# A hybrid transformer block on one core: a written order held longer in the first seven-product block, and x loaded ahead of the small parameters

## The chip, the cores and the metric

The kernel runs on one core of one Trainium2 chip, as one launch. The metric is the device time of that launch in microseconds (us). Five engines work side by side, each through a queue of its own: TensorE (PE, matmuls into PSUM banks), VectorE (DVE), ScalarE (ACT), GpSimd (POOL) and SyncE (SP), which here issues all DMAs. An engine takes its queue in order; an instruction that waits for a semaphore holds up all that stand behind it on that engine.

## The reference, cut to what matters

One layer of a transformer block over 512 tokens of width 1024, in float32, modulated by a condition vector `c`:

```python
mod = jax.nn.silu(c) @ w_ada[l] + b_ada[l]
sh1, sc1, g1, sh2, sc2, g2 = jnp.split(mod[:, None, :], 6, axis=-1)
hn = (_rms(x, norm1_g[l]) * (1 + sc1) + sh1).astype(x.dtype)
y = _mixer(hn, w_in[l], ...)
x = x + g1 * (y.astype(x.dtype) @ w_out[l])
hn = (_rms(x, norm2_g[l]) * (1 + sc2) + sh2).astype(x.dtype)
gate, up = jnp.split(hn @ w_gate_up[l], 2, axis=-1)
x = x + g2 * ((jax.nn.silu(gate) * up) @ w_down[l])
```

`_rms` divides each row by the root of its mean square. The mixer projects `hn` by `w_in` and runs softmax heads with a forget gate, mLSTM heads and block-sparse softmax heads. The gate and up projection has 2 x 2816 columns.

## The kernel before

Every matmul of a projection is done three times, on high and low parts of its operands: an operand is rounded by ScalarE to a high part (names that end in `h`), and VectorE subtracts that from the operand to make the low part (names in `l`).

**The start.** SP issues the loads in the order of the code: first three small ones, `c` (`cT`, 4 KB), a packed table of norm gains, biases and convolution weights (`prmT`, 44 KB) and the gate biases (`gbias`, 7 KB); then the four row tiles of x, 512 KB each (`x0` to `x3`, 128 tokens each); then the slices of `w_ada` and `w_in` for the first projection. ScalarE computes `cs`, the SiLU of `c`. The row sums of x squared are split: x0, x2 and half of x3 on ScalarE, x1 and the other half of x3 on VectorE; a chain of small VectorE instructions makes of the four sums the reciprocal roots `rs`, and both engines scale the rows by them (`xscale`). TensorE does some matmuls on `sq2`, a square of x, that are there to keep it busy, then transposes x and multiplies with `cs`.

**The gate and up projection.** It is cut into 11 blocks `q` of 256 gate columns and their 256 up columns. Block 0 is done plainly (`plain`, banks `fp`). Blocks 1 to 10 are done by a scheme that needs seven matrix products in place of eight; the seven are called phases and run in the order 1, 2, 6, 5, 7, 4, 3. A product is 24 matmuls of 256 columns. Its weights are raw tiles or sums of raw tiles: block `q` has raw tiles `r{q}00`, `r{q}01`, `r{q}11`, `r{q}10`, loaded in this order, and VectorE makes of them in place `r{q}00` (phase 5), `r{q}t` (phase 6), `r{q}01` (phase 7) and `r{q}10` (phase 4). `split` then makes `fw{q}{phase}h` on ScalarE and `fw{q}{phase}l` on VectorE. Products 6 and 7 go on accumulating in the bank `f{q}A` of phase 1, and product 3 in the bank `f{q}C` of phase 5, so each must wait until the bank has been copied or read (`u16`, `u17`, `u15`). Phases 1 and 2 of blocks 1 and 2 are done early, ahead of block 0; of these blocks five products are left. Block 0's own SiLU and product (`plain_glu`: `fps0`, `fps1` on ScalarE, `A0` on VectorE), and the last of the split operands (`os40`, `os41`), are written between the preparation of phase 7 of block 1 and what follows. `f1C` takes a bank that `fps1` reads.

**What sets the order.** A scheduler places the instructions of each engine. The class `_InOrder` (line 104) wraps each engine; while its switch `in_order[...]` is 1, each instruction gets a dependence on the one written before it, so the engine's queue keeps the written order, and while it is 0 the scheduler is free. The switches for VectorE and ScalarE are 1 through the start, then 0, and 1 again from line 1270, after block 0's matmuls. The loop over products runs the preparation two products ahead:

```python
    for i, (q, ph) in enumerate(run):
        upto = todo.index(run[min(i + AHEAD, len(run) - 1)])
        while ahead <= upto:
            prepare(*todo[ahead])
            ...
            if todo[ahead] == (1, 7):
                plain_glu(0)
                for g_ in range(2):
                    operand("s4", g_, s4[g_])
                plain_glu(1)
                in_order["V"][0] = in_order["S"][0] = 0
            ahead += 1
        product(q, ph)
        after(q, ph)
```

So before, the two switches go to 0 once phase 7 of block 1 is prepared.

Of the kernel before, what the change touches and what calls it, by code (L numbers as in the profile page):

```python
# [11 lines left out]
AF = mybir.ActivationFunctionType  # L12
ALU = mybir.AluOpType
# [3 lines left out]
P = 128  # L17
# [113 lines left out]
def hybrid_block_kernel(  # L131
# [6 lines left out]
    V, S, G, TE, SY = nc.vector, nc.scalar, nc.gpsimd, nc.tensor, nc.sync  # L138
    dbg = dbg or {}
    in_order = {k: [1] for k in "VSGTY"}  # L140
    V, S, G, TE, SY = (_InOrder(tc, e, in_order[k]) for e, k in zip((V, S, G, TE, SY), "VSGTY"))
# [33 lines left out]


    cT = cp.tile([P, 8], F32, name="cT")
    SY.dma_start(cT, c[0].rearrange("(p k) -> p k", k=8))
    prmT = cp.tile([P, NPRM], F32, name="prmT")
    SY.dma_start(prmT, prm)  # L180
    gbias = cp.tile([P, 14], F32, name="gbias")
    SY.dma_start(gbias, gate_b.partition_broadcast(P))

    cs = cp.tile([P, 8], F32, name="cs")
    S.activation(cs, cT, AF.Silu)
    b1sc = cp.tile([P, 2, 8], F32, name="b1sc")
    V.tensor_scalar(b1sc[:, 0, :], prmT[:, 8:16], 1.0, None, op0=ALU.add)
    V.tensor_scalar(b1sc[:, 1, :], prmT[:, 32:40], 1.0, None, op0=ALU.add)
    gq8 = cp.tile([P, 2], F32, name="gq8")
    V.tensor_scalar(gq8[:, 0:1], prmT[:, 84:85], -0.125, None, op0=ALU.mult)  # L190
    V.tensor_scalar(gq8[:, 1:2], prmT[:, 86:87], -0.125, None, op0=ALU.mult)

    w_ada_v = w_ada[0].rearrange("(p k) n -> p k n", k=8)

# [64 lines left out]
    with ExitStack() as s0:  # L259
# [7 lines left out]
        def load_kc(kc):  # L267

            a_ = box["ada", kc] = ap_.tile([P, 8, 2, P], F32, tag="ada", name=f"ada{kc}", bufs=ADB)
            for i in range(2):  # L270
                SY.dma_start(a_[:, :, i, :], w_ada_v[:, :, i * D + kc * P:i * D + kc * P + P])
            ws = box["ws", kc] = wp.tile([P, 512], F32, tag="ws", name=f"w0s{kc}", bufs=WS)
            SY.dma_start(ws, w_in[0, kc * P:(kc + 1) * P, MQK:MQK + 512])

        for t in range(NT):
            xx = xp.tile([P, D], F32, name=f"x{t}")
            SY.dma_start(xx, x[0, t * P:(t + 1) * P, :])
            xt.append(xx)
        for kc in range(ADB - 1):
            load_kc(kc)  # L280
        sq = [ap_.tile([P, D], F32, tag=f"sq{t % 2}", name=f"sq{t}", bufs=1) for t in range(NT)]

        def square(t, o, acc):

            if acc == "S":
                S.activation(sq[t][:, o], xt[t][:, o], AF.Square, accum_out=ss[:, t:t + 1])
            else:
                V.tensor_tensor_reduce(out=sq[t][:, o], in0=xt[t][:, o], in1=xt[t][:, o], op0=ALU.mult,
                                       op1=ALU.add, scale=1.0, scalar=0.0, accum_out=acc)

        gT = [bank("g", f"gT{m}") for m in range(4)]
        def xscale(t, c0, c1):
            if t % 2:
                S.activation(xt[t][:, c0:c1], xt[t][:, c0:c1], AF.Copy, scale=rs[:, t:t + 1])
            else:
                V.tensor_scalar(xt[t][:, c0:c1], xt[t][:, c0:c1], rs[:, t:t + 1], None, op0=ALU.mult)
# [3 lines left out]
        ssx = cp.tile([P, 1], F32, name="ssx")  # L300
        square(NT - 1, slice(0, D // 2), "S")
        square(NT - 1, slice(D // 2, D), ssx)
        V.tensor_tensor(ss[:, NT - 1:NT], ss[:, NT - 1:NT], ssx, op=ALU.add)
        V.tensor_scalar(v1, ss, 1.0 / D, EPS, op0=ALU.mult, op1=ALU.add)
        for f in rsqrt_ops(rs, v1, "n4"):
# [3 lines left out]
            TE.matmul(gT[3][:, 0:256], ident, sq[2][:, 0:256], start=True, stop=True)  # L309
        for t in range(NT):  # L310
            xscale(t, 0, XS)

        def px_(kc):
            px = box["px", kc] = bank("s", f"px{kc}")
            for t in range(NT):
                TE.transpose(px[:, t * P:(t + 1) * P], xt[t][:, kc * P:(kc + 1) * P], ident)
# [726 lines left out]
    def operand(name, g_, src):  # L1043

        mk = act_tile if name in ("22", "s1", "s3") else op_tile
        h_, l_ = (mk(f"o{name}{g_}{c}").rearrange("p (a b) -> p a b", a=2) for c in "hl")
        S.activation(h_, src, AF.Copy)
        V.tensor_tensor(l_, src, f32(h_), op=ALU.subtract)
        for i in range(2):
            so[name, 2 * g_ + i] = h_[:, i, :], l_[:, i, :]  # L1050
# [49 lines left out]
    def temp(name):  # L1100
        return act_tile(name, F32)
# [26 lines left out]
    def prepare(q, ph):  # L1128

        if ph == 1 and q + 1 < NQ:  # L1130
            load(q + 1)
        if ph in (1, 2):
            if (q, ph) not in wts:
                split(q, ph, raw[q, ph - 1, 0])
            return
        if ph == 6:
            ffn["sums"] = sums(q)
        if ph in (6, 7, 4):
            next(ffn["sums"])
        split(q, ph, {6: raw[q, "t2"], 5: raw[q, 0, 0], 7: raw[q, 0, 1], 4: raw[q, 1, 0], 3: raw[q, 1, 1]}[ph])  # L1140

    def product(q, ph):
        bk = BANK[ph]
        first = ph not in (6, 7, 3)
        if first:
            pbk[q, bk] = bank(TAG[bk], f"f{q}{bk}")
        pb = pbk[q, bk]
        for kp in range(4):
            wh, wl = wts[q, ph][kp]
            sh, sl = so[OPS[ph], kp]  # L1150
            for f in range(2):
                cs_ = slice(P * f, P * f + P)
                o = pb[:, 256 * f:256 * f + 256]
                last = kp == 3
                TE.matmul(o, wh[:, cs_], sh, start=first and kp == 0 and f == 0, stop=False, skip_group_check=True)
                TE.matmul(o, wh[:, cs_], sl, start=False, stop=False, skip_group_check=True)
                TE.matmul(o, wl[:, cs_], sh, start=False, stop=last, skip_group_check=True)
# [6 lines left out]
    def after(q, ph):  # L1164
        pb = pbk[q, BANK[ph]]
        if ph in (1, 6, 7):
            t_ = tmp[q, ph] = temp(f"u{q}{ph}")
            S.activation(t_, pb, AF.Copy)
        if ph == 2:
            V.tensor_tensor(tmp[q, 1], pb, tmp[q, 1], op=ALU.add)  # L1170
        elif ph == 7:
            pc = pbk[q, "C"]
            t_ = tmp[q, 5] = temp(f"u{q}5")
            V.tensor_tensor(t_, pc, tmp[q, 7], op=ALU.add)
        elif ph == 4:
            V.tensor_tensor(tmp[q, 7], tmp[q, 7], pb, op=ALU.subtract)
            glu(q, 1, tmp[q, 7], tmp[q, 5])
        elif ph == 3:
            V.tensor_tensor(tmp[q, 6], pb, tmp[q, 6], op=ALU.add)
            glu(q, 0, tmp[q, 1], tmp[q, 6])  # L1180
# [53 lines left out]
    def plain_glu(hb):  # L1234
        g_, u_ = pbank[hb]
        t_ = temp(f"fps{hb}")
        S.activation(t_, g_, AF.Silu)
        V.tensor_tensor(ffn["A"][0][:, :, 256 * hb:256 * hb + 256], u_.rearrange("p (a b) -> p a b", a=2),
                        t_.rearrange("p (a b) -> p a b", a=2), op=ALU.mult)
# [36 lines left out]
    def down_load(n):  # L1276
        for hf_, j in DP[len(draw):n]:
            r_ = draw[hf_, j] = fp.tile([P, 2, 512], F32, tag="raw", name=f"dr{hf_}{j}", bufs=RAW)
            SY.dma_start(r_, w_down[0, j * P:(j + 2) * P, 512 * hf_:512 * hf_ + 512].rearrange(
                "(a p) n -> p a n", p=P))  # L1280
# [15 lines left out]
    todo = [(q, ph) for q in range(1, NQ) for ph in PHASES]  # L1296
    run = [k for k in todo if k[0] > NE or k[1] > 2]
    ahead = 0
# [4 lines that stand above are left out]
            if todo[ahead] == (NQ - 1, 1):  # L1303
                down_load(4)
            if todo[ahead] == (1, 7):
                plain_glu(0)
                for g_ in range(2):
                    operand("s4", g_, s4[g_])
                plain_glu(1)
                in_order["V"][0] = in_order["S"][0] = 0  # L1310
            ahead += 1
        product(q, ph)
        after(q, ph)
# [72 lines left out]
```

## Time and profile before

| | |
|---|---|
| median of 3 runs | 685.63 us (684.65 to 687.03) |
| the profiled execution's own time | 685.51 us |
| its span in the trace | 683.8 us |
| TensorE's mean granted clock | 0.995 of full speed |
| busy: TensorE, VectorE, ScalarE, GpSimd | 650.5, 518.4, 363.9, 95.7 us |

The span is that of one execution; some 1.7 us of the time lie around it. Busy time says little about what a stage is worth: the table shows TensorE at work nearly throughout, and the places where it waits have to be looked up one by one.

### The profile page before, as it was taken

What the parts mean: (1) busy time and instruction counts of PE and PEld (TensorE: products, weight loads), DVE (VectorE), ACT (ScalarE), POOL (GpSimd) and SP (SyncE); (2) the same over time, 40 slices, a digit from 0 to 9 for tenths busy, and PEclk for the clock granted to TensorE, in tenths of its full rate; (3) what the DMA queues carried; (4) which work ended last, traced back from release to release, by engine and by line L of the source; (5) the groups of instructions that cost most, each with busy time, mean ns of one, the idle gap of its engine ahead of it and who ended that gap; (6) DMA issues with size and microseconds to landing.
All of it is one profiled execution on the core that took longest, in us unless ns stands there. A gap on an engine that the chain in (4) does not pass through costs nothing.

```text
span 683.8 us, 11780 instructions
## 1 busy us (share of the span) xinstructions
PE 650.5 (95%) x4238; PEld 587.4 (86%) x4238; DVE 518.4 (76%) x1034; ACT 363.9 (53%) x721; POOL 95.7 (14%) x130
## 2 busy tenths in 40 slices
PE   3999998999999999999996999999999999999997
PEld 2678887899999987788996999999999998788885
DVE  3539888979998899888749778887777999448313
ACT  3435487656876777637824445444544665226210
POOL 2012225245253264000000000000000000000000
PEclk9999999999999999999998999999999999999999
DMA  8986736667877776622715433223333237405101
GB/s 261 305 240 173 184 93 158 162 169 210 203 215 181 181 208 181 214 63 62 231 35 181 125 124 120 63 75 114 124 124 125 79 116 226 166 15 205 58 0 61
DMA packets 95549, 99.64 MB, mean 146 GB/s; under 512 B 8186, under 2 KB 70010, under 8 KB 95492
## 3 DMA queue, kind: packets, MB, share of 16 engines
q1 hardware_dynamic: 95492, 98.91, 49.9%
q8 instruction: 33, 0.54, 0.3%
q14 instruction: 24, 0.20, 0.1%
HBM read 84.15 MB, written 2.10 MB: 126 GB/s over the span
## 4 chain that ended last, share of the span: by engine, by line
PE 72%; DVE 15%; DMA 4%; ACT 4%; issue 4%; SPq 1%; DVEq 0%; ACTq 0%
PE d L114 14%; PE B L114 6%; PE F L114 6%; PE fp L114 3%; PE ol L114 3%; PE gT L114 3%; DVE g L114 1%; PE pc L114 1%; PE f9A L114 1%; PE f8A L114 1%; PE f7A L114 1%; PE f6A L114 1%; PE f5A L114 1%; PE f3A L114 1%; PE f4A L114 1%
## 5 line engine op out<-in xcount | busy, mean ns | idle before, releaser
L114 ACT ACTIVATE ah<-A 128x512 fp32r<-128x512 f32 x44 | 25.5, 620 | 33.4 <-PE d L114 33.1
L114 DVE TENSOR_TENSOR al<-A,ah 128x512 fp32r<-128x512 f32 x44 | 29.0, 682 | 18.1 <-ACT ah L114 18.1
L114 DVE TENSOR_TENSOR r<-r,r 128x1024 f32<-128x1024 f32 x20 | 24.3, 1219 | 9.5 <-DMA r<-in_w_gate_up_dram 9.2
L114 DVE TENSOR_TENSOR fo<-d,g1b 128x512 f32<-128x512 f32 (+1 forms) x9 | 5.6, 630 | 17.9 <-PE d L114 17.8
L114 ACT ACTIVATE Fp<-Fs,Fmn 128x128 f32<-128x128 f32 (+3 forms) x24 | 12.6, 527 | 9.6 <-DVE Fmn L114 5.6
L114 ACT ACTIVATE Bp<-Bs,Bmn 128x128 f32<-128x128 f32 (+3 forms) x24 | 12.6, 527 | 6.9 <-DVE Bmn L114 4.4
L114 DVE SCALAR_TENSOR_TENSOR m<-pc,b1sc,prmT 128x1 f32<-128x1 f32 x8 | 1.7, 218 | 19.0 <-PE pc L114 19.0
L114 POOL TENSOR_SCALAR Fp<-Fp,Fls 128x128 f32<-128x128 f32 (+2 forms) x18 | 11.9, 664 | 26.4 <-DVE Fls L114 17.2
L114 PE MATMUL gT<-sq,ident 128*128 128x256 f32 x12 | 5.1, 614 | 10.4 <-ACT sq L114 10.4
L114 ACT ACTIVATE u<-u 128x512 f32<-128x512 f32 x20 | 12.5, 626 | 2.8 <-DVE u L114 2.6
L114 DVE TENSOR_TENSOR A<-u,u 128x512 f32<-128x512 f32 x20 | 13.7, 683 | 0.0
L114 PEld LDWEIGHTS gT<-sq,ident 128*128 128x128 f32 x12 | 3.9, 331 | 11.3 <-issue 10.4
L114 POOL TENSOR_SCALAR Bp<-Bp,Bls 128x128 f32<-128x128 f32 (+2 forms) x16 | 8.7, 542 | 34.4 <-DVE Bls L114 28.1
L114 DVE TENSOR_TENSOR Bptl<-Bpt,Bpth 128x128 fp32r<-128x128 f32 (+3 forms) x24 | 11.5, 484 | 1.8 <-ACT Bpth L114 1.5
L114 DVE CUSTOM_DVE_ANT_0 Bs<-Bs,mask 128x128 f32<-128x128 f32 (+3 forms) x24 | 11.6, 491 | 1.6 <-PE Bs L114 1.5
L114 ACT ACTIVATE Fpth<-Fpt 128x128 fp32r<-128x128 f32 (+3 forms) x24 | 10.4, 435 | 4.1 <-PE Fpt L114 4.0
L114 DVE CUSTOM_DVE_ANT_0 Fs<-Fs,mask 128x128 f32<-128x128 f32 (+3 forms) x24 | 11.7, 487 | 1.0 <-PE Fs L114 1.0
L114 PE MATMUL Bpt<-ident,Bp 128*128 128x128 f32 x60 | 10.8, 277 | 1.7 <-DVE Fyp L114 0.7
L114 POOL TENSOR_TENSOR sml<-E,smh 128x512 fp32r<-128x512 f32 (+1 forms) x8 | 9.0, 1127 | 23.7 <-ACT smh L114 17.3
L114 DVE TENSOR_TENSOR Fptl<-Fpt,Fpth 128x128 fp32r<-128x128 f32 (+3 forms) x24 | 11.6, 483 | 0.6 <-ACT Fpth L114 0.4
L114 ACT ACTIVATE Bpth<-Bpt 128x128 fp32r<-128x128 f32 (+3 forms) x24 | 10.3, 434 | 3.1 <-PE Bpt L114 2.9
L114 ACT ACTIVATE row<-pc 128x256 f32<-128x256 f32 x8 | 3.1, 382 | 15.6 <-PE pc L114 15.6
(2324 smaller groups left out, 2823.9 us busy)
## 6 DMA issues: line engine op xcount, KB each, us to landing
r<-in_w_gate_up_dram SPq DMA_DIRECT2D x40, 512.0 KB, 4.6
dr<-in_w_down_dram SPq DMA_DIRECT2D x22, 512.0 KB, 5.3
ada<-in_w_ada_dram SPq DMA_DIRECT2D x16, 512.0 KB, 7.3
x<-in_x_dram SPq DMA_DIRECT2D x4, 512.0 KB, 4.6
w0s<-in_w_in_dram SPq DMA_DIRECT2D x8, 256.0 KB, 6.6
g10s<-in_w_ada_dram SPq DMA_DIRECT2D x8, 256.0 KB, 3.9
g11s<-in_w_ada_dram SPq DMA_DIRECT2D x8, 256.0 KB, 2.9
sc20s<-in_w_ada_dram SPq DMA_DIRECT2D x8, 256.0 KB, 4.1
```

What stands on the lines that cost most here:

```text
L114: r = f(*a, **k)
```

## The change

Two things. First, the switches of VectorE and ScalarE go to 0 later: not after phase 7 of block 1 but after phase 6 of block 2 is prepared, so that both engines keep the written order through the whole of block 1's five products. Second, the loads of `cT`, `prmT` and `gbias` are issued behind the four loads of x; `cs` is computed behind the squares, and the four VectorE instructions on `prmT` (`b1sc`, `gq8`) behind the first scaling.

```diff
     cT = cp.tile([P, 8], F32, name="cT")
-    SY.dma_start(cT, c[0].rearrange("(p k) -> p k", k=8))
     prmT = cp.tile([P, NPRM], F32, name="prmT")
-    SY.dma_start(prmT, prm)
     gbias = cp.tile([P, 14], F32, name="gbias")
-    SY.dma_start(gbias, gate_b.partition_broadcast(P))
...
-    S.activation(cs, cT, AF.Silu)
...
-    V.tensor_scalar(b1sc[:, 0, :], prmT[:, 8:16], 1.0, None, op0=ALU.add)
...
             SY.dma_start(xx, x[0, t * P:(t + 1) * P, :])
             xt.append(xx)
+        SY.dma_start(cT, c[0].rearrange("(p k) -> p k", k=8))
+        SY.dma_start(prmT, prm)
+        SY.dma_start(gbias, gate_b.partition_broadcast(P))
...
         square(NT - 1, slice(D // 2, D), ssx)
+        S.activation(cs, cT, AF.Silu)
...
             xscale(t, 0, XS)
+        V.tensor_scalar(b1sc[:, 0, :], prmT[:, 8:16], 1.0, None, op0=ALU.add)
...
                 plain_glu(1)
+            if todo[ahead] == (2, 6):
                 in_order["V"][0] = in_order["S"][0] = 0
```

VectorE's queue at the beginning of block 1, before (`r200` is the first sum of block 2, `r110` block 1's for phase 4):

```order
L114 TENSOR_TENSOR r1t_4877<-r111_4883,r100_4879 128x1024
L114 TENSOR_TENSOR r200_4887<-r201_4889,r200_4887 128x1024
L114 TENSOR_TENSOR r110_4885<-r1t_4877,r110_4885 128x1024
L114 TENSOR_TENSOR fw16l_4898<-r1t_4877,fw16h_4897 128x1024
L114 TENSOR_TENSOR fw15l_4902<-r100_4879,fw15h_4901 128x1024
L114 TENSOR_TENSOR r101_4881<-r111_4883,r101_4881 128x1024
L114 TENSOR_TENSOR r201_4889<-r211_4891,r201_4889 128x1024
L114 TENSOR_TENSOR fw17l_4907<-r101_4881,fw17h_4906 128x1024
```

The same place in the change, on to the first low part of block 2:

```order
L114 TENSOR_TENSOR r1t_4877<-r111_4883,r100_4879 128x1024
L114 TENSOR_TENSOR fw16l_4898<-r1t_4877,fw16h_4897 128x1024
L114 TENSOR_TENSOR fw15l_4902<-r100_4879,fw15h_4901 128x1024
L114 TENSOR_TENSOR r101_4881<-r111_4883,r101_4881 128x1024
L114 TENSOR_TENSOR fw17l_4907<-r101_4881,fw17h_4906 128x1024
...
L114 TENSOR_TENSOR fw13l_4981<-r111_4883,fw13h_4980 128x1024
L114 TENSOR_TENSOR u15_5010<-f1C_4955,u17_5008 128x512
L114 TENSOR_TENSOR r200_4887<-r201_4889,r200_4887 128x1024
L114 TENSOR_TENSOR r2t_5020<-r211_4891,r200_4887 128x1024
L114 TENSOR_TENSOR u17_5008<-u17_5008,f1D_5027 128x512
L114 TENSOR_TENSOR r201_4889<-r211_4891,r201_4889 128x1024
L114 TENSOR_TENSOR fw26l_5024<-r2t_5020,fw26h_5023 128x1024
```

`r200`, `r110` and `r201` have moved behind the low parts that stood after them; the sums of block 2 now stand behind `u15`. ScalarE's queue over the same stretch, in the change (before, `fw14h` stood between `os40h` and `os41h`, and `fw26h` and `fw25h` ahead of `u17`):

```order
L114 ACTIVATE fw17h_4906<-r101_4881 128x1024
L114 ACTIVATE fps0_4910<-fp00_4612 128x512
L114 ACTIVATE os40h_4913<-s40_4852 128x512
L114 ACTIVATE os41h_4917<-s41_4858 128x512
L114 ACTIVATE fps1_4921<-fp10_4726 128x512
L114 ACTIVATE u16_4948<-f1A_4407 128x512
L114 ACTIVATE fw14h_4951<-r110_4885 128x1024
L114 ACTIVATE fw13h_4980<-r111_4883 128x1024
L114 ACTIVATE u17_5008<-f1A_4407 128x512
L114 ACTIVATE fw26h_5023<-r2t_5020 128x1024
L114 ACTIVATE u17_5008<-u17_5008 128x512
L114 ACTIVATE fw25h_5055<-r200_4887 128x1024
```

`fw14h` comes later, `fps1` no longer has it ahead. And ScalarE's queue at the very start of the program, in the change; before, there was one table load, and `cs` stood right behind it:

```order
L114 ACT_TABLE_LOAD
L114 ACTIVATE sq_164,ss<-x_133 128x1024
L114 ACTIVATE sq_166,ss<-x_137 128x1024
L114 ACTIVATE sq_167,ss<-x_139 128x512
L114 ACT_TABLE_LOAD
L114 ACTIVATE cs<-cT 128x8
L114 ACTIVATE x_135<-x_135,rs 128x384
```

`cs` now stands between the squares and the scaling, and a second load of ScalarE's function tables has come in ahead of it. TensorE's queue changes only in which few matmuls of neighbouring products stand first; from block 4 on, no engine's order differs.

## Rows read from the trace of the kernel before

**Rows 1.** The page, busy time by engine: busy us, share of the span, instructions.

```profile
PE 650.5 (95%) x4238; PEld 587.4 (86%) x4238; DVE 518.4 (76%) x1034; ACT 363.9 (53%) x721; POOL 95.7 (14%) x130
```

**Rows 2.** Waits of TensorE, whole span: total us, times, longest us.

```profile
PE gT L114 <- ACT sq L114: 10.4, 1, 10.4
PE f1A L114 <- DVE fw16l L114: 5.5, 1, 5.5
PE ms L114 <- DMA K<-mkh: 1.4, 1, 1.4
```

**Rows 3.** Windows: length, busy us by engine, granted clock, DMA share, GB/s.

```profile
382.00:548.00 166.00, 166.00 (x1386) 166.00 (x1385) 137.91 (x145) 84.46 (x103) 0.00 (x0) 1.00 0.33 105
548.00:586.00 38.00, 37.25 (x194) 31.23 (x194) 36.19 (x52) 21.61 (x33) 0.00 (x0) 1.00 0.61 196
```

**Rows 4.** Timeline, VectorE: start, us, instruction, idle before and releaser.

```profile
349.07 1.23 DVE L114 TENSOR_TENSOR r1t<-r,r 128x1024 f32<-128x1024 f32 x1
359.52 1.22 DVE L114 TENSOR_TENSOR r<-r,r 128x1024 f32<-128x1024 f32 x1 [9.22 <-DMA r<-in_w_gate_up_dram]
360.66 1.22 DVE L114 TENSOR_TENSOR r<-r1t,r 128x1024 f32<-128x1024 f32 x1
361.80 1.22 DVE L114 TENSOR_TENSOR fw16l<-r1t,fw16h 128x1024 fp32r<-128x1024 f32 x1
...
367.55 0.68 DVE L114 TENSOR_TENSOR A<-fp,fps 128x512 f32<-128x512 f32 x1
```

**Rows 5.** Timeline, ScalarE, the same stretch (the two fps are fps0 and fps1).

```profile
350.39 1.06 ACT L114 ACTIVATE fw16h<-r1t 128x1024 fp32r<-128x1024 f32 x1 [5.16 <-DVE r1t L114]
...
365.31 1.06 ACT L114 ACTIVATE fw17h<-r 128x1024 fp32r<-128x1024 f32 x1 [12.92 <-DVE r L114]
366.28 0.58 ACT L114 ACTIVATE fps<-fp 128x512 f32<-128x512 f32 x1
...
368.74 0.58 ACT L114 ACTIVATE fps<-fp 128x512 f32<-128x512 f32 x1
```

**Rows 6.** The chain that ended last, 355 to 400 us: start, us, what.

```profile
355.88 3.61 DMA r<-in_w_gate_up_dram
...
369.38 3.13 PE f1C L114 x24
...
392.59 2.88 PE f2C L114 x24
```

**Rows 7.** Timeline, TensorE, around its wait in block 1.

```profile
357.13 0.28 PE L114 MATMUL f1A<-os20h,fw16h 128*128 128x256 f32 x1
357.25 0.28 PE L114 MATMUL f1A<-os20l,fw16h 128*128 128x256 f32 x1
363.07 0.58 PE L114 MATMUL f1A<-os20h,fw16l 128*128 128x256 f32 x1 [5.54 <-DVE fw16l L114]
```

**Rows 8.** Windows of the same stretch, columns as in rows 3.

```profile
358.00:360.00 2.00, 0.00 (x0) 0.00 (x0) 0.48 (x1) 0.00 (x0) 0.00 (x0) 0.95 1.07 376
...
366.00:368.00 2.00, 1.52 (x10) 1.32 (x9) 2.00 (x3) 2.00 (x4) 0.00 (x0) 0.84 0.72 226
```

**Rows 9.** Timeline of SP's queue and of ScalarE at the start.

```profile
0.79 0.39 SPq L114 DMA_DIRECT2D cT<-in_c_dram  x1
...
2.18 1.85 SPq L114 DMA_DIRECT2D x<-in_x_dram  x4
...
0.79 1.28 ACT L114 ACT_TABLE_LOAD   x1 [0.79 <-PEq L1375]
2.42 0.21 ACT L114 ACTIVATE cs<-cT 128x8 f32<-128x8 f32 x1 [0.34 <-DMA cT<-in_c_dram]
...
10.47 0.63 ACT L114 ACTIVATE sq<-x 128x512 f32<-128x512 f32 x1 [0.20 <-DMA x<-in_x_dram]
...
13.90 1.12 ACT L114 ACTIVATE x<-x,rs 128x384 f32<-128x384 f32 x2 [2.71 <-DVE rs L114]
```

**Rows 10.** Window of the first projection, columns as in rows 3.

```profile
20.00:48.00 28.00, 27.95 (x199) 20.42 (x200) 13.02 (x33) 10.73 (x20) 0.00 (x0) 1.00 1.03 272
```

More of the change, by code (lines that the diff above doesn't have):

```diff
@@ L177, in hybrid_block_kernel @@
     cT = cp.tile([P, 8], F32, name="cT")
-    SY.dma_start(cT, c[0].rearrange("(p k) -> p k", k=8))
     prmT = cp.tile([P, NPRM], F32, name="prmT")
-    SY.dma_start(prmT, prm)
     gbias = cp.tile([P, 14], F32, name="gbias")
-    SY.dma_start(gbias, gate_b.partition_broadcast(P))
     cs = cp.tile([P, 8], F32, name="cs")
-    S.activation(cs, cT, AF.Silu)
     b1sc = cp.tile([P, 2, 8], F32, name="b1sc")
-    V.tensor_scalar(b1sc[:, 0, :], prmT[:, 8:16], 1.0, None, op0=ALU.add)
-    V.tensor_scalar(b1sc[:, 1, :], prmT[:, 32:40], 1.0, None, op0=ALU.add)
     gq8 = cp.tile([P, 2], F32, name="gq8")
-    V.tensor_scalar(gq8[:, 0:1], prmT[:, 84:85], -0.125, None, op0=ALU.mult)
-    V.tensor_scalar(gq8[:, 1:2], prmT[:, 86:87], -0.125, None, op0=ALU.mult)
     w_ada_v = w_ada[0].rearrange("(p k) n -> p k n", k=8)
@@ L311, in hybrid_block_kernel @@
             xscale(t, 0, XS)
+        V.tensor_scalar(b1sc[:, 0, :], prmT[:, 8:16], 1.0, None, op0=ALU.add)
+        V.tensor_scalar(b1sc[:, 1, :], prmT[:, 32:40], 1.0, None, op0=ALU.add)
+        V.tensor_scalar(gq8[:, 0:1], prmT[:, 84:85], -0.125, None, op0=ALU.mult)
+        V.tensor_scalar(gq8[:, 1:2], prmT[:, 86:87], -0.125, None, op0=ALU.mult)
         def px_(kc):
```

## The prediction

> **What bounds the kernel now.** I read the page first: TensorE is busy 650.5 of 683.8 us [rows 1]. Then who waits for whom on TensorE, whole span: two waits stand far above the rest, 10.4 us at the start for the first squares and 5.5 us for `fw16l`; the next is 1.4 us [rows 2]. The change touches the code around both. The windows show what follows: from 382 to 548 us TensorE is busy 166.00 of 166.00 us, from 548 to 586 it is 37.25 of 38.00 [rows 3]. So work that reaches TensorE earlier at 382 us ends earlier by as much, unless VectorE, busy 137.91 and 36.19 us in these windows, falls behind.
>
> The 5.5 us are a wait behind a wait. VectorE makes `r1t`, the sum that phase 6 of block 1 uses, by 350.30; ScalarE rounds it to `fw16h` from 350.39 to 351.45. Then VectorE does nothing until 359.52: the next instruction in its queue is `r200`, a sum of block 2, and one of its inputs is a DMA that is issued at 355.88 and takes 3.61 us [rows 4, 5, 6]. `fw16l`, with all its inputs at 351.45, stands two places behind and starts at 361.80 [rows 4]. TensorE does the two matmuls that need only `fw16h` at 357.13 and 357.25, and the third at 363.07 [rows 7]. The granted clock falls meanwhile: a mean of 0.95 in 358 to 360 (so it went to 0.5, 1.2 GHz, at 359.8) and of 0.84 in 366 to 368 (back to 2.4 GHz at 366.6) [rows 8]. ScalarE's chain trails too: `fw17h` at 365.31 after 12.92 us of idle time, `fps1` at 368.74, and only behind that `f1C` at 369.38 [rows 5, 6].
>
> **The change, part by part: the block.** The 24 matmuls of a product take 2.88 us at full clock, and the last product of block 2, `f2C` of phase 3, ends at 392.59 + 2.88 = 395.47 [rows 6]. From 357.13 to there stand ten products, 28.8 us; 38.3 us pass. So 9.5 us are lost there, and that is the most this part can return.
>
> What the new order leaves of it I work out in steps. A 1,024-wide VectorE instruction takes 1.22 us, and the next starts 1.14 after it (360.66, 361.80); a 512-wide one takes 0.68, and I let the next start after 0.60 [rows 4]. On ScalarE the wide one takes 1.06 with the next start after 0.97 (365.31, 366.28), the narrow one 0.58, and I take 0.5 to the next [rows 5]. A dependent starts some 0.03 to 0.09 us after the end that it waits for.
> - VectorE: `fw16l` 351.5 to 352.7, `fw15l` to 353.8, `r101` to 355.0; ScalarE `fw17h` to 356.1; VectorE `fw17l` to 357.3. All this lies in VectorE's former idle time, under the plain product. TensorE then runs phase 6 of block 1 from 357.13 to 360.0 without a gap.
> - ScalarE's first SiLU, `fps0`, reuses a buffer that the end of the plain product reads, so I let it start at 357.3. Behind it stand `os40h`, `os41h` and `fps1`, which ends at 359.4. `f1C` needs the bank that `fps1` reads, at 360.0: covered by 0.6 us.
> - VectorE: the two `A0` and the two `os4` tails to 360.4, `r110` to 361.5; ScalarE `fw14h` to 362.6; `fw14l` to 363.8, wanted at 365.8, when phases 5 and 7 are through. `fw13l` to 365.0, wanted at 368.7.
> - Now what the written order costs. `u15` waits for ScalarE's copy `u17` of the bank after phase 7 (365.8), so VectorE stands from 365.0 to 366.6 with the sums of block 2 behind it. `u15`, `r200`, `r2t`, `u17`, `r201` take it to 371.2, `fw26l` from there to 372.5. TensorE ends block 1 at 371.53. Four matmuls can go ahead of `fw26l` (two on `fw26h`, two on `fw25h`, ready at 372.1), so some 0.5 us stays open. Block 2's weights are in by then: the DMA of 355.88 lands at 359.5, and the two behind it, 1 MB, take 2.8 us at the 376 GB/s of rows 8.
> - Block 2 ends at 371.53 + 0.5 + 14.4 = 386.4. Is VectorE late for block 3? From 372.4 on it has eleven wide instructions (12.5 us) and eight narrow ones (4.8) up to `fw36l`, 389.7, and TensorE wants that two products later, at 392.2. The 2.5 us between cover its waits, and in the steady stretch it needs only 137.91 of 166 us, so the lead comes back [rows 3].
>
> Gain: 395.47 - 386.4 = 9.0 us. Bounds: 9.5 if nothing stays open, 7.5 if the dependents trail by another 1.5 us.
>
> **The start.** The four loads of x were issued from 2.18 us on, and now take the place that `cT` had, 0.79: 1.39 us earlier [rows 9]. The half square of x3 waits for the last of them and starts at 10.47; on the four row sums hang the small VectorE instructions to `rs`, and on these the scaling at 13.90 [rows 9]. TensorE's warm-up matmuls hang on a square of x too (the 10.4 us of rows 2). All of it moves by 1.39.
>
> The three small loads now stand behind x in the same queue: 55 KB by their shapes, 0.2 us at the 272 GB/s of the stretch [rows 10]. The weight loads behind them are issued no later than before, so these gain 1.2 us. From 20 to 48 us TensorE is busy 27.95 of 28.00 us [rows 10]: it sets the pace there and waits for no weights. I take 1.3 us, between 1.2 and 1.39.
>
> What the moved instructions cost. `cs` now stands on ScalarE between the last square, which ends at 10.47 + 0.63 and with the reading of its sum at some 11.2 - 1.39 = 9.8, and the scaling, at 13.90 - 1.39 = 12.5, and a second table load stands ahead of it. The load of before took 1.28 us and `cs` 0.21 [rows 9]: done at 11.3, hidden by 1.2 us; without that cover 1.5 us would be on the path. The Trainium skill, "ScalarE: Activation LUTs", section "What ACT_TABLE_LOAD costs", gives a switch 1.28 us and a drain of another 1.38; by that `cs` ends at 12.7, the scaling starts 0.2 us late, and the sum would be 0.2 us more. Here `cs` stood idle 0.34 us behind the load, for its DMA [rows 9], which bears out the first part alone. `cT` took 1.6 us from issue to `cs` in an empty queue (0.79 to 2.42); set behind the last x at 9.1 it is there by 10.7 even if nothing overlaps, and it holds up the scaling only from 12.3 on. The four small instructions on `prmT` go behind VectorE's part of the scaling, where it waits for TensorE's first columns anyway, and `gbias` is read only in the next stage.
>
> **Sum.** 685.51 - 9.0 - 1.3 = 675.2 us, on the profiled execution's own time (span 683.8). That lies 0.12 us under the median of the three runs, so the number stands for the median as well.
>
> **Rivals.**
> 1. Only the block pays (chance 0.15). For: the start's gain must pass some 300 us of projection and attention with many small waits, and the second table load or a late `cT` could eat it. Against: those waits are for engines that move along. 685.51 - 9.0 = 676.5.
> 2. A gap stays that is long enough for the clock (0.10). Before, the clock fell at 359.8, some 2.4 us after TensorE's last matmul, and came back at 366.6, 3.5 us after the restart, which costs half of that, 1.8 us. If `fps1` or `fw26l` came 2.5 us after TensorE wants it, the loss is 2.5 + 1.8 - 0.5 = 3.8 us: 679.0. For: the cover ahead of `f1C` is only 0.6 us, that ahead of `f2A` negative. Against: 2 us more would have to be missing in steps whose lengths the rows give.
> 3. The wait only moves (0.04). Block 2's sums, early before because they stood ahead, come behind `u15`, and `f2A` waits as `f1A` did. With 8 us or more of that: 683.5 to 685.5. Against: the five instructions from `u15` up to `fw26l` start 4.6 us ahead of it at their full pace, and TensorE has 5.8 us of block 1 left when phase 7 ends.
> 4. Slower (0.03): the same place, but `fw26l` later than 372.5 + 10.3 = 382.8; every us after that is lost. With a gap of twice the old 5.5 us and the half clock, 12.8 us, it is 675.2 + 12.8 = 688.0. That needs the copy `u17` to be held for some 12 us by what stands ahead of it on ScalarE, `fw14h` and `fw13h`; both have their inputs by 362.6.
>
> **How the numbers follow.** The forecast has 0.68, with a range of its own from 674.6 (9.5 and 1.39) to 676.7 (7.5 and 1.3). The range of 674.0 to 679.0 takes in rival 1 and the nearer half of rival 2 and leaves out rivals 3 and 4; 0.6 us at the low end is for what repeated runs differ by. About 0.3%, 2.06 us, is what a measurement of this kernel tells from no change: faster than 683.6 are the forecast and rivals 1 and 2, 0.93; within it rival 3, 0.04; slower rival 4, 0.03.
>
> **What would show it.** Right: VectorE idle no more after `r1t`, `fw16l` near 351.5 less the start's gain, `f1A`'s third matmul 0.12 after its second, the clock at 1.00 there, the half square of x3 at 9.1, a TensorE gap under 1 us ahead of `fw26l`. Wrong: a wait of `f1C` on `fps1` or of `f2A` on `fw26l` over 2 us with the clock at 0.50; a scaling of x that starts behind `cs`; a first transpose that comes 1.4 us earlier and a block 1 that doesn't move with it.

## The result, and the profile after

The change takes 675.71 us (median of 4 runs, 674.96 to 676.92) against 686.33 for the kernel before in the same comparison: ratio 0.985, interval 0.9825 to 0.9876, so 1.2 to 1.8% faster. The profiled execution took 675.63 us, with a span of 673.8. The forecast was 675.2. Two executions, one of 1059.87 us with the release at (2, 2) and one of 1620.27 with the release at (2, 3), are left out of the medians below.

The page's line of busy time after (before: [rows 1]): TensorE does the same 4238 matmuls in 2.4 us less, and the span is 10.0 us shorter.

```profile
PE 648.1 (96%) x4238; PEld 585.9 (87%) x4238; DVE 517.7 (77%) x1034; ACT 365.0 (54%) x722; POOL 95.1 (14%) x130
```

TensorE's waits after, first the largest of the whole span, then all of 345 to 400 us (total, times, longest). Against [rows 2] the wait for `fw16l` is gone, that for the first squares is 1.9 us shorter, and one is new: `pc` on `ada`, the first slices of `w_ada`.

```profile
PE gT L114 <- ACT sq L114: 8.5, 1, 8.5
PE pc L114 <- DMA ada<-in_w_ada_dram: 1.6, 1, 1.6
...
PE f2C L114 <- ACT fw25h L114: 0.4, 1, 0.4
```

VectorE at the beginning of block 1, after (start, length, idle before; compare [rows 4]):

```profile
347.94 1.23 DVE L114 TENSOR_TENSOR r1t<-r,r 128x1024 f32<-128x1024 f32 x1
350.35 1.23 DVE L114 TENSOR_TENSOR fw16l<-r1t,fw16h 128x1024 fp32r<-128x1024 f32 x1 [1.18 <-ACT fw16h L114]
...
365.53 0.69 DVE L114 TENSOR_TENSOR u<-f1C,u 128x512 f32<-128x512 f32 x1 [1.71 <-ACT u L114]
366.14 1.22 DVE L114 TENSOR_TENSOR r<-r,r 128x1024 f32<-128x1024 f32 x1
...
370.26 1.22 DVE L114 TENSOR_TENSOR fw26l<-r2t,fw26h 128x1024 fp32r<-128x1024 f32 x1
```

The idle time of 9.22 us behind `r1t` has become 1.18, the time in which ScalarE rounds `r1t`. `fw16l` ends at 351.58; TensorE, which begins block 1 at 356.00, wants it at 356.24, so it has 4.7 us to spare:

```profile
356.00 0.28 PE L114 MATMUL f1A<-os20h,fw16h 128*128 128x256 f32 x1
...
356.24 0.28 PE L114 MATMUL f1A<-os20h,fw16l 128*128 128x256 f32 x1
```

`r200` now starts at 366.14, behind `u15`, and no longer waits for a load (block 2's were issued from 354.76 on). ScalarE over the same stretch (compare [rows 5]; the two fps are fps0 and fps1):

```profile
353.88 1.06 ACT L114 ACTIVATE fw17h<-r 128x1024 fp32r<-128x1024 f32 x1 [2.61 <-DVE r L114]
356.08 0.60 ACT L114 ACTIVATE fps<-fp 128x512 f32<-128x512 f32 x1 [1.14 <-PE fp L114]
...
357.61 0.59 ACT L114 ACTIVATE fps<-fp 128x512 f32<-128x512 f32 x1
```

`fps1` ends at 358.20 and `f1C` starts at 359.04 in the chain that ended last (start, length, what; compare [rows 6]):

```profile
356.16 2.88 PE f1A L114 x24
359.04 2.88 PE f1C L114 x24
361.92 2.89 PE f1A L114 x24
...
371.23 0.51 PE f2C L114 x2
371.74 2.69 PE f2A L114 x22
...
382.83 2.88 PE f2C L114 x24
```

Every product of block 1 takes its 2.88 us: no half clock, no wait. The one opening is the 0.4 us that `f2C` waits for `fw25h`; from there the chain runs back over `fw26h`, `r2t` and `r200` to `u15`. Block 2 ends at 385.71 instead of 395.47. After that VectorE keeps its lead (windows, columns as in [rows 3]):

```profile
382.00:538.00 156.00, 156.00 (x1302) 156.00 (x1302) 132.47 (x140) 79.64 (x97) 0.00 (x0) 1.00 0.33 107
538.00:576.00 38.00, 37.53 (x197) 31.48 (x197) 36.34 (x52) 21.61 (x33) 0.00 (x0) 1.00 0.60 192
```

The start after: SP's queue and ScalarE (compare [rows 9]), and then TensorE's first two `pc`, in the trace of before and after.

```profile
0.80 1.82 SPq L114 DMA_DIRECT2D x<-in_x_dram  x4
...
8.53 0.63 ACT L114 ACTIVATE sq<-x 128x512 f32<-128x512 f32 x1
...
9.27 1.28 ACT L114 ACT_TABLE_LOAD   x1
10.56 0.21 ACT L114 ACTIVATE cs<-cT 128x8 f32<-128x8 f32 x1
11.96 1.12 ACT L114 ACTIVATE x<-x,rs 128x384 f32<-128x384 f32 x2 [1.19 <-DVE rs L114]
```

```profile
15.91 1.07 PE L114 MATMUL pc<-ada,cs 128*32 128x256 f32 x16
...
18.51 1.07 PE L114 MATMUL pc<-ada,cs 128*32 128x256 f32 x16
```

```profile
13.94 1.07 PE L114 MATMUL pc<-ada,cs 128*32 128x256 f32 x16
...
18.19 1.07 PE L114 MATMUL pc<-ada,cs 128*32 128x256 f32 x16 [1.58 <-DMA ada<-in_w_ada_dram]
```

x is used 1.94 us earlier (the half square of x3 at 8.53 instead of 10.47, the scaling at 11.96 instead of 13.90), the first `pc` 1.97, the second only 0.32: it waits for its weights. The windows of 8.0 to 9.5 us show why; the last column is GB/s, the one ahead of it the DMA share.

```profile
8.00:8.50 0.50, 0.00 (x0) 0.00 (x1) 0.00 (x0) 0.38 (x2) 0.00 (x0) 1.00 0.11 18
8.50:9.00 0.50, 0.47 (x1) 0.50 (x2) 0.42 (x1) 0.47 (x1) 0.00 (x0) 1.00 0.03 4
9.00:9.50 0.50, 0.50 (x2) 0.34 (x1) 0.40 (x3) 0.48 (x3) 0.00 (x0) 1.00 0.63 164
```

Behind the last of x the DMA engines stand nearly idle for 1 us, at 18 and 4 GB/s, ahead of the first weights. Before, x is still coming in there, at 418, 401 and 370 GB/s, and no such stretch follows it: 317 to 345 GB/s from 9.5 to 11.0 us.

For x the 1.94 us are the best of six traces. In five of the kernels below the loads stand as in the change up to the first `gbias`; there the half square starts at 8.98 to 9.31, which is 1.16 to 1.49 us earlier than before.

### The profile page after: what moved, and what is told of

Its sections match the earlier page's. It is cut to its first block, busy times and chain, and to the rows that moved or that the text cites. A ratio compares the mean times of both kernels' runs of the same rounds, so it can differ in the third digit from the quotient of the medians.

```text
span 673.8 us, 11777 instructions
## 1 busy us (share of the span) xinstructions
PE 648.1 (96%) x4238; PEld 585.9 (87%) x4238; DVE 517.7 (77%) x1034; ACT 365.0 (54%) x722; POOL 95.1 (14%) x130
## 4 chain that ended last, share of the span: by engine, by line
PE 71%; DVE 15%; DMA 4%; issue 4%; ACT 4%; SPq 1%; POOL 0%; DVEq 0%; ACTq 0%; POOLq 0%
PE d L114 14%; PE B L114 5%; PE F L114 5%; PE ol L114 4%; PE fp L114 3%; PE gT L114 3%; DVE g L114 2%; PE f9A L114 1%; PE f8A L114 1%; PE f7A L114 1%; PE f6A L114 1%; PE f5A L114 1%; PE f4A L114 1%; PE f3A L114 1%; PE pc L114 1%
```

## The experiments

Two questions: which part of the change pays, and by which mechanism. In the block the theory is the head of the line (`fw16l` waited behind `r200`, and `r200` for a DMA), against the rest of the new order. At the start it is what the small loads cost behind x. Ratios are to the kernel before, run in the same comparison.

**The block alone.** The kernel before, with the release of the written order moved as in the change.

```diff
             if todo[ahead] == (1, 7):
...
                 plain_glu(1)
+            if todo[ahead] == (2, 6):
                 in_order["V"][0] = in_order["S"][0] = 0
```

> Only the longer written order; the loads at the start stand as in the kernel before. If the two parts simply add, as the shift of TensorE's instructions in the changed kernel says (about 1.0 us won before block 1, 8.8 us in it), this runs some 8.9 us under the kernel before and 1.0 us over the changed one: about 676.7 us, ratio 0.987, with the wait before f1A gone. Rival, that the earlier start is eaten on the way and the whole gain is the block's: 675.7 us, ratio 0.9855, the same as the change.

Measured: 676.59 us (675.90 to 678.38), ratio 0.988 (0.9866 to 0.9894). The first theory's ratio of 0.987 lies in this interval, the rival's 0.9855 just outside. There is no wait for `fw16l`, and block 2 ends at 387.18 instead of 395.47:

```profile
357.64 2.88 PE f1A L114 x24
...
384.30 2.88 PE f2C L114 x24
```

`f1A` stands 1.48 us behind the one after, and so does the end of block 2. From `f1A`'s first matmul (357.47) to there it takes 29.71 us, as after the change (356.00 to 385.71): the block gives the same with or without the start. The start here is that of the kernel before, whose `f1A` began at 357.13; by 0.34 us two traces with the same start differ here.

**The start alone.** The change, with the release back at (1, 7).

```diff
             if todo[ahead] == (1, 7):
...
                 plain_glu(1)
-            if todo[ahead] == (2, 6):
                 in_order["V"][0] = in_order["S"][0] = 0
```

> Only the moved loads; the written order ends after phase 7 of block 1 as before. Parts that add: 1.0 us under the kernel before, about 684.9 us, ratio 0.9985, with the first scaling near 12.0 us as in the changed kernel and the second weight tile waited for, and f1A's wait of 5.5 us still there. Rival, start eaten on the way: the scaling is earlier but the total is that of before, 685.9 us, ratio 1.000.

Measured: 685.29 us (683.50 to 690.44), ratio 1.0005 (0.9987 to 1.0023): by itself the start is worth nothing that can be measured. Its trace is 0.92 us ahead of the kernel before at the last plain product, and loses that in the block. Windows (granted clock third from the end) and one piece of the chain:

```profile
360.00:362.00 2.00, 0.00 (x0) 0.00 (x0) 2.00 (x2) 0.00 (x0) 0.00 (x0) 0.50 0.44 148
...
366.00:368.00 2.00, 1.03 (x7) 0.67 (x6) 2.00 (x4) 2.00 (x5) 0.00 (x0) 1.00 0.59 197
368.00:370.00 2.00, 1.50 (x9) 1.45 (x9) 2.00 (x4) 1.93 (x4) 0.00 (x0) 0.74 0.78 251
370.00:372.00 2.00, 2.00 (x11) 2.00 (x11) 1.97 (x3) 0.00 (x0) 0.00 (x0) 0.50 0.77 237
```

```profile
368.55 4.63 PE f1C L114 x24
```

The clock was back at full in 366 to 368 and fell to half a second time, in 368 to 372; the 24 matmuls of `f1C` take 4.63 us, against 3.13 in [rows 6]. Those 1.5 us are more than the start had gained. So the two parts don't add, and in this trace the gain is lost in a patchy stretch. For the other runs that is not shown: three more of the twelve have a mean granted clock as low as the profiled one's (0.991 or less) and take 686.52 to 690.44 us, but the eight others, at 0.993 to 0.995, have a median of 684.64, only 0.4 us under the kernel before.

**The head of the line.** The change, with the release just ahead of the step that prepares phase 6 of block 2.

```diff
-            if todo[ahead] == (2, 6):
+            if todo[ahead] == (2, 2):
                 in_order["V"][0] = in_order["S"][0] = 0
```

All of block 1's steps stay in written order; only the sums of block 2 are free, and the scheduler puts `r200` right behind `r1t` again. (In the list of steps (2, 2) stands directly ahead of (2, 6), so this is one step ahead of the change and four behind the kernel before; the expectation miscounts that.)

> The change, but the written order is given up one step after the kernel before did it (after phase 2 of block 2 is prepared, the next in the list, in place of phase 6): VectorE's queue has `r200` behind `r1t` again and `r201` ahead of `fw17l`, the other moved instructions (`r110`, `fps1` ahead of `fw14h`) stay where the change puts them. Theory A, the block's gain is that `fw16l` no longer stands behind `r200`, which waits for a DMA: `r200` starts near 358.5 us, `fw16l` near 359.7 and ends at 360.9, TensorE wants it at 356.3, so a gap of 4.6 us returns and with it a half clock that costs up to 1.8 us; the 0.4 us ahead of `f2A` go away: 680 to 682.5 us. Theory B, the rest of the written order makes the gain (the low parts in the order in which TensorE wants them): no gap over 1 us, 675 to 676.5 us.

Measured: 684.28 us, ratio 0.9977 (0.9959 to 0.9994); four runs lie at 681.49 to 682.86, five at 684.28 to 685.45, above theory A's range. The wait is back: `f1A` for `fw16l`, 4.4 us, behind an idle time of 9.26 on VectorE. But the profiled run, 684.28, was also late before the block: it had waited 1.71 us for `ada` at 18 us, and its granted clock was 0.50 in the window from 20 to 24. The next kernel takes that wait away.

```diff
         SY.dma_start(prmT, prm)
-        SY.dma_start(gbias, gate_b.partition_broadcast(P))
...
             load_kc(kc)
+        SY.dma_start(gbias, gate_b.partition_broadcast(P))
...
-            if todo[ahead] == (2, 6):
+            if todo[ahead] == (2, 2):
```

> The kernel that gave up the written order one step later than before (`r200` ahead of `fw16l` again; it ran at 681.5 to 682.9 us in four runs and at 684.3 to 685.5 in five), with `gbias` behind the first four weight tiles. Theory A, the two groups of times come from the start, where the wait for `ada` let the clock fall in its profile: without that wait all runs lie in the lower group or under it, 680.5 to 683 us, and the profile's clock is at full from 12 to 28 us. Theory B, the groups come from the block, from a second fall of the clock behind the wait for `fw16l`: they stay, 681.5 to 685.5 us.

Measured: 681.52 us, ratio 0.9936 (0.9916 to 0.9956); eight runs at 679.77 to 682.51, two at 684.09 and 684.96. The clock is 1.00 from 12 to 28 us in its profile. The upper group has shrunk from five of nine to two of ten, and the two ratios' intervals lie apart, so part of it came from the start. Theory A wanted all runs in the lower group; what the last two came from stays open, since neither was profiled. TensorE's waits from 340 to 400 us, a window, block 1's first matmul and two pieces of the chain:

```profile
PE f1A L114 <- DVE fw16l L114: 4.5, 1, 4.5
PE f1C L114 <- ACT fps L114: 0.4, 1, 0.4
```

```profile
360.00:362.00 2.00, 2.00 (x10) 2.00 (x10) 2.00 (x3) 0.04 (x1) 0.00 (x0) 0.50 0.04 9
```

```profile
354.76 0.28 PE L114 MATMUL f1A<-os20h,fw16h 128*128 128x256 f32 x1
```

```profile
365.08 3.14 PE f1C L114 x24
...
388.38 2.88 PE f2C L114 x24
```

The same kernel with the release after (2, 6) is the one with `gbias` late, below: 675.45 us. The place of `r200` (and of `r201`, which moves with it) is thus worth 6.1 us of the time (5.8 by the two ratios, which differ by 0.0084). Between the traces it is 6.8: from `f1A`'s first matmul to the end of block 2 it takes 36.50 us here (354.76 to 391.26) and 29.71 there. The theory of the head of the line holds; the other orders inside block 1 give the smaller part.

**How much cover the block has.** The change, with 4 or 8 more instructions on VectorE ahead of `fw16l`.

```diff
             if (q, ph) == (1, 6):
+                for _ in range(4):
+                    V.tensor_tensor(g1b, g1b, g1b, op=ALU.max)
```

> The change with four more 1,024-wide VectorE instructions (in place, on a table of gains, 1.14 us each, 4.6 us together) ahead of `fw16l`, which measures what cover the block has. Theory A, `fw16l` alone is what block 1 waited for: it ends at 356.2 us in place of 351.6, TensorE wants it at 356.3, and the time stays at 675.7 us within 0.7. Theory B, the next thing to be late is `fps1`: `r101`, `fw17h`, `fps0` and `fps1` trail by the delay less ScalarE's 1.1 us of idle time, `fps1` ends near 361.6 us, `f1C` wants it at 359.0, so TensorE waits 2.6 us there: 678.3 us, and up to 680.1 with a half clock.

Measured: 677.91 us, ratio 0.9917 (0.9885 to 0.9949), three runs within 677.68 to 678.10 and the profiled one at 683.40, which lost its clock twice before the block (0.69 in 20 to 24 us, behind a wait of 1.7 us for `ada`, and 0.50 in 120 to 124). What its block shows still tells the two theories apart, in the chain:

```profile
362.95 1.06 ACT fw17h L114
364.00 0.48 ACT fps L114
...
365.52 0.49 ACT fps L114
...
366.06 3.14 PE f1C L114 x24
```

TensorE no longer waits for `fw16l` but 1.6 us for `fps1`, through `r101`, `fw17h` and `fps0`. The three other runs have a median of 677.72, 2.0 us above the change; theory B said 2.6. It had left out VectorE's idle time of 1.18 us behind `r1t`: counted from `f1A`'s first matmul (361.41 here, 356.00 after the change) `fw16l`, which starts at 359.42, came 3.7 us later and not 4.6.

> The same with eight instructions, 9.1 us. Theory A: `fw16l` ends at 360.7 us, a gap of 4.4 us ahead of `f1A`'s third matmul, the granted clock falls to half about 2.4 us after the last matmul as in the kernel before, and costs up to 1.8 us more: 680 to 682 us. Theory B: the same gap, and a second one ahead of `f1C`, which `fps1` (ending near 366.2 us) now holds up until 7.2 us after the time in the change: 682.9 us without the clock's share, up to 685 with it.

Measured: 682.80 us, ratio 0.9978 (0.9962 to 0.9995). TensorE waits 3.9 us for `fw16l`, the clock is 0.50 from 360 to 364 us, and `f1C` then waits 0.3 us for `fps1`. `f1C` starts 9.69 us after `f1A`'s first matmul (365.26 and 355.57) instead of 3.04, 6.65 us later; theory B had 7.2. The time is between the theories: the gap and the half clock stand one behind the other, but they give `fps1` the time to catch up, so the second gap that B added is all but covered.

**Further than the change.** With `gbias` late, and the written order held through the whole of block 2.

```diff
-            if todo[ahead] == (2, 6):
+            if todo[ahead] == (2, 3):
```

> The kernel with `gbias` behind the first four weight tiles (675.45 us when run before), and the written order given up after phase 3 of block 2 in place of phase 6, with which `fw26l` stands right behind `r2t`, ahead of `u17` and `r201`. Theory A, each wait that TensorE has left there is worth its length: the 0.4 us ahead of `f2A` close, 675.0 us. Theory B, what is gained at the start and at that place is taken back by waits at other places, VectorE being at 132.5 of 156 us there: 675.4 to 676 us, no different from the change.

Measured: 679.61 us, ratio 0.9919 (0.9905 to 0.9933), 4.2 us slower than with the release after (2, 6). Neither theory had that. Of the 0.4 us ahead of `f2A` 0.2 stay, now for `fw26l`, and worse waits open in the next two products; ScalarE and the chain:

```profile
377.03 1.06 ACT L114 ACTIVATE fw27h<-r 128x1024 fp32r<-128x1024 f32 x1 [3.39 <-DVE r L114]
```

```profile
379.40 4.40 PE f2A L114 x22
```

`fw27h`, at 371.08 after the change, comes at 377.03: its sum `r201` starts at 375.69 instead of 369.13, behind the two `A` sums of block 1 and `fw25l`. TensorE waits in pieces of 1.3, 0.3, 0.3 and 0.2 us, and the 22 matmuls take 4.40 us instead of 2.64, in good part at the half clock (0.50 in 380 to 382). So rival 3's mechanism, that the wait only moves, is real in this kernel, at phase 7 of block 2, two products further on than it was put.

**The small loads, from another queue.** The change, with the three issued by ScalarE.

```diff
-        SY.dma_start(cT, c[0].rearrange("(p k) -> p k", k=8))
-        SY.dma_start(prmT, prm)
-        SY.dma_start(gbias, gate_b.partition_broadcast(P))
+        S.dma_start(cT, c[0].rearrange("(p k) -> p k", k=8))
+        S.dma_start(prmT, prm)
+        S.dma_start(gbias, gate_b.partition_broadcast(P))
```

> The changed kernel with the three small loads issued from ScalarE's queue at the very start instead of from SP's behind x. In the changed kernel the DMA engines are nearly empty from 8.0 to 9.1 us, between x and the first weight tile, and TensorE waits 1.58 us for the second weight tile. Theory A, the small loads in the same queue make the hole: it goes, the weights come about 1 us earlier, the wait shrinks to 0.6 us or less, and the time is some 0.9 us under the changed kernel, about 674.8 us. Theory B, the weight tile is late for reasons of its own (its many small pieces): hole and wait stay, 675.7 us.

Measured: 676.51 us (676.19 to 677.89), ratio 0.9879 (0.9866 to 0.9891). Theory A's hole and wait come out (TensorE waits 0.4 us for `ada`), but not its time. The weights are now issued at 2.65 us, and the idle stretch behind x is gone, but another slow one has come inside x: from 6.0 to 8.5 us the DMA engines move 100 to 223 GB/s, with 401 ahead of it and 387 behind. x itself comes later: the half square of x3 starts at 11.02, later than before the change.

```profile
11.02 0.63 ACT L114 ACTIVATE sq<-x 128x512 f32<-128x512 f32 x1 [1.00 <-DMA x<-in_x_dram]
```

The Trainium skill, "DMA: Bandwidth & Descriptors", section "Issuing engines are not separate DMA queues", says that loads of all issuing engines share the 16 engines and interleave; the 11.02 here, against 8.53 to 9.31 where all three stand behind x in SP's queue, fits that. How much of it is the small loads and how much the earlier weights this run does not tell.

**`gbias` behind the first weights.** The change, with that one load (one row of 14 numbers to all 128 partitions) moved.

```diff
         SY.dma_start(prmT, prm)
-        SY.dma_start(gbias, gate_b.partition_broadcast(P))
...
             load_kc(kc)
+        SY.dma_start(gbias, gate_b.partition_broadcast(P))
```

> The changed kernel with only the gate-bias load moved further back, behind the first four weight tiles. If that load, a broadcast of one row to 128 partitions, makes the hole between x and the first weight tile, the hole shrinks from 1.1 us to under 0.3 and the wait for the second weight tile from 1.58 to about 0.7: 674.8 us. If all three small loads share in it, a third of that: 675.4 us. If it is the weight tile's own: no change, 675.7 us.

Measured: 675.45 us (673.50 to 675.81), ratio 0.9852 (0.9836 to 0.9868). The idle stretch and the wait for `ada` are gone:

```profile
8.00:8.50 0.50, 0.00 (x0) 0.00 (x0) 0.00 (x0) 0.50 (x1) 0.00 (x0) 1.00 1.00 297
8.50:9.00 0.50, 0.00 (x0) 0.00 (x0) 0.00 (x0) 0.39 (x2) 0.00 (x0) 1.00 1.14 337
```

```profile
17.57 1.07 PE L114 MATMUL pc<-ada,cs 128*32 128x256 f32 x16
```

The second `pc` starts 0.62 us earlier than after the change, and block 2 ends 0.46 earlier, at 385.25; the half square of x3, at 9.11, lies among those of the traces with the change's order. So this load made the stretch, as the first theory has it, and the two others, still behind x, don't. In the time this can't be told from the change.

**`gbias` twice.** The change, with that load doubled into a tile that nothing reads.

```diff
         SY.dma_start(gbias, gate_b.partition_broadcast(P))
+        gbias2 = cp.tile([P, 14], F32, name="gbias2")
+        SY.dma_start(gbias2, gate_b.partition_broadcast(P))
```

> The change with the gate biases loaded a second time, into a tile that nothing reads, right behind the first such load: the suspected spacer in the stream of loads is doubled. Theory A, this broadcast load is what leaves the DMA engines nearly idle ahead of the weights, and the wait that it makes is what lets the clock fall in some runs (with waits of 1.1 and 1.6 us on `ada` it stayed at full in the profiles, with 1.7 twice it fell): TensorE's wait for `ada` grows from 1.6 to 2.3 us or more, the granted clock falls to half between 19 and 25 us, and the time is 678 to 681 us. Theory B, the spacer comes of the change from x to weights in the stream, whatever stands between: the wait stays at 1.1 to 1.7 us, and the time at 675 to 677.5 us.

Measured: 678.27 us (677.26 to 679.08), ratio 0.9886 (0.9867 to 0.9906), 2.6 us above the change; the second `pc` starts 1.82 us later, at 20.01. The stretch of nearly idle DMA engines lasts from 8.0 to 10.5 us, at 48 to 4 GB/s, instead of 8.0 to 9.0, and TensorE's wait for `ada` to 2.4 us in two pieces:

```profile
9.00:9.50 0.50, 0.50 (x1) 0.44 (x2) 0.46 (x1) 0.50 (x1) 0.00 (x0) 1.00 0.05 4
9.50:10.00 0.50, 0.50 (x3) 0.38 (x2) 0.40 (x3) 0.48 (x3) 0.00 (x0) 1.00 0.05 5
10.00:10.50 0.50, 0.50 (x3) 0.41 (x2) 0.40 (x4) 0.50 (x1) 0.00 (x0) 1.00 0.07 10
```

So such a load is a spacer of 1 to 1.5 us for 7 KB. The time is that of theory A, but not by its clock: that stayed at 1.00 from 12 to 28 us, with more waiting than where it had fallen.

## Why the prediction was right, step by step

**The bound and the mechanism.** Right. The 5.5 us of [rows 2] were a wait behind a wait, and the load at their head was itself released by TensorE's plain product: the chain goes from it, at 355.87, to the issue at 355.88 [rows 6]. Putting `r200` back ahead of `fw16l` brings 4.4 to 4.5 us of them and the half clock back, 6.1 us of the time.

**The block, 9.0 us.** Right, and 0.4 too much. From the first matmul of `f1A` (357.13 before, 356.00 after) to the end of block 2 it took 38.34 us before and takes 29.71 now: 8.6. The terms between traces, each by the run that shows it: `r200` and `r201` 6.8; `r110` ahead of `fw16l` 1.0 (`f1A`'s gap of 5.54 us in [rows 7] is 4.54 with `r200` alone); `fw14h` ahead of `fps1` 0.9 (from `f1A`'s third matmul to `f1C` 6.31 us before and 5.38 with the order of block 1 kept). These make 8.7, all of it within 0.1; the last two were not tried alone. What stays open ahead of `f2A` is 0.67 us in the chain (block 1 would end at 370.56, and `f2C`'s first piece starts at 371.23) instead of 0.5; the rest is the time a last matmul needs beyond the step to the next, which the sum left out.

**The steps inside it.** `fw16l` was put at 351.5 less the start's gain and started at 350.35. The cover of `f1C` was put at 0.6 us and is 0.84. `u15` was put at 366.6 and started at 365.53, 1.1 earlier with everything else. `fw26l` was put at 371.2 and started at 370.26. VectorE's lead in block 3 came back as worked out: no wait in 372 to 538 us.

**The start, 1.3 us.** Half right, and its size in the time is not shown. x was put 1.39 us earlier, the half square at 9.1; in six traces of that start it comes at 8.53 to 9.31, in the middle as worked out (the 1.94 of the change's own trace is the best of them). The term that failed is the other one, the weights' gain of 1.2 us, 1.39 less "0.2 us at the 272 GB/s": a rate of large loads set for small ones, where the small loads left the engines nearly idle for 1 us. The weights were not issued earlier but 0.35 us later (4.42, before 4.07), and the second `pc`, which waits for them, starts at 18.19 to 18.59 in the five of these traces with one `gbias`, against 18.51 and 18.30 with the start of before. The "waits for no weights" was read from 20 to 48 us [rows 10]; the wait of 1.58 us came ahead of that. How TensorE gains behind it all the same was not taken apart: at the third `pc` (23.05) the change is 0.94 us ahead of the kernel before, but only 0.26 ahead of the block alone. At the first matmul of `f1A` the start's gain is 1.13 us between the two main traces, 0.92 and 1.48 between the pairs with one part alone, and the start alone shows nothing in the time. So that the sum came so near is partly luck.

**ScalarE's second table load.** Right: 1.28 us, `cs` 0.01 us behind its end, done at 10.77, and the scaling started 1.19 us after that, when `rs` was there. The drain of 1.38 us that the Trainium skill adds in "ScalarE: Activation LUTs", section "What ACT_TABLE_LOAD costs", and the 0.2 us that would have come of it, do not show here.

**The rivals.** Rival 1 describes the block alone, which ran at 676.59 where 676.5 was worked out; the change, 0.9 us under it, is not told from it by its time (the intervals overlap), only by its trace, where the block starts earlier. So of the forecast and rival 1 the times don't settle which it was. Rivals 2 to 4 did not come: `fps1` was not late, and all that TensorE waited ahead of `f2A` was 0.4 us for `fw25h`. Rival 2's gap of 2.5 us is no condition, though: with the release at (2, 3) the clock fell to half behind waits of 1.3 us and less, while it stayed at full behind the 1.6 us of the four added instructions. The delays of 4 and 8 instructions show how near rival 2 was: 4.6 us of added work made 1.6 us of wait, so the cover is some 3 us, and `fps1` uses it up before `fw16l` does.

**The sum.** 685.51 - 8.6 - 1.1 = 675.8, and 0.3 us more come back behind the blocks (the long run of `d` in the chain starts at 574.98 instead of 585.02, 10.04 earlier, block 2 ended 9.76 earlier); the profiled run took 675.63.

## What to carry to other kernels

Where an engine stands idle for long, look not at what it waits for but at what stands behind the waiting instruction: here 9.2 us of VectorE went to a sum that was wanted a whole block later. Here it paid to hold the written order just past the first work that waits for something slow, and no further: of the places tried, one step earlier cost 6.1 us, four steps later 4.2. A gain ahead of a stretch with gaps is not safe until the gaps are closed; in one and the same order of loads x came up to 0.8 us apart from trace to trace, so such a gain wants several; and a small load is costed by the time the DMA engines stand idle around it, not by its bytes.

## What the runs showed of the hardware

- A load that gives one row of 56 bytes to 128 partitions, 7 KB, left the DMA engines nearly idle for about 1 us when it stood between two large loads (4 and 18 GB/s in the change; 12 to 56 in the slowest half us of four other traces), and two of them for about 2.5 us. Moved behind the first weights it left no such stretch.
- The granted clock, half after a wait of 5.6 us and back at full, fell to half a second time, in a stretch where TensorE was busy 1.03 of 2.00 us and then 1.50 of 2.00 (one trace, with the start alone). In the kernel before it stayed at full through 1.12 of 2.00, in 368 to 370 us.
- Behind a wait of 1.7 us at 18 us the clock fell to half in two profiles, in kernels whose code is the same there; behind waits of 1.6 us, and of 2.4 us in two pieces, it stayed at full. What decides that stays open; a kernel without the wait did not show it.
